# Side streams that run further in front: filters, convolutions and token sums placed anew in the Hyena stage of a single-core inference step

## The chip, the cores and the metric

One core of a Trainium2 chip runs the whole step. The metric is the device time of one execution in microseconds. The engines are named as in the profile: PE is the matrix engine, PEld its weight loads, DVE the vector engine, ACT the scalar engine, POOL and SP two further engines, of which POOL and SP here mostly issue DMAs. Each engine takes its instructions in one fixed order, and waits on semaphores for the others.

## The reference

One layer of a hybrid backbone for two groups of tokens: 128 prompt tokens and 512 sample tokens, 640 in all, 1024 channels, float32. What bears on the change is the Hyena branch:

```python
h = x * (1 + scale) + shift
z = h @ w_in                                   # 1024 -> 10240 columns
hy = short_conv(hy, conv_w, conv_b)            # 3 taps along the tokens
v_h, x1, x0 = jnp.split(hy, 3, axis=-1)

def hyena_long_conv(v_h, x1, x0, h_fwd, h_bwd, d_bias):
    u = v_h * x1
    ...
    uf = jnp.fft.rfft(u.astype(jnp.float32), n=n, axis=1)
    ff = jnp.fft.rfft(filt_full, n=n, axis=0)
    y = jnp.fft.irfft(uf * ff[None], n=n, axis=1)[:, :L].astype(u.dtype)
    return (y + u * d_bias) * x0
```

The filter (`filt_full`) comes from a small network with a decay. The other branch is neighbourhood attention for the samples and plain attention for the prompt. Both are gated, projected, merged, projected out and normalised.

## The kernel before

All products are done with operands split into a high and a low part (`split`: a copy on ACT makes the high part, a subtraction on DVE the low part), so one product is three passes of PE: high by high, low by high, high by low (`mm3`).

**The stage.** The change touches the stage from about 60 to 370 us. Its main stream is the projection `h @ w_in` in tiles of 128 output channels (`conv_tile`, in the profile `mm`, for PE 48 matmuls of 128x320) and in blocks of values (`v`, `ve`). The 1024 Hyena channels go in four quarters of two tiles. `quarter_head(q)` makes `u` (tile n) and `x1` (tile 8+n) and multiplies them; `quarter_tail(q)` makes `x0` (tile 16+n). A tile's way is: two of four PSUM banks (`mm_0`, `mm_1`) are filled by PE; ACT copies them out to a padded row `zs0` or `zs1`, in turn, with four copies (L481 to L485); ACT does the middle tap (L487) and DVE the two outer taps (L489, twice, reading `zs`). The next tile's copies into the same `zs` wait for the second of these DVE passes, and the next matmuls into the same banks wait for the copies.

**The side streams.** `filter_spectrum(q)` makes the filter of a quarter and its transform: five classes of rows (`fl`), decay on DVE (`sd`), split (`sh`, `sl`), transform as products with cosine and sine matrices (`fa`, `fb`, `fc`, `fd`, `fp`), sums into `F`. `long_conv(q)` transposes `u` (`ut`), splits it (`uh`, `ul`), transforms it (`c_X`, `s_X`, `p_X`), combines to `X` and multiplies with `F` (`W`). `long_conv_back(q)` splits the product (`ph`, `pl`), transforms back (`yb`), transposes (`yp`, `y`), and adds `u * d_bias` (L633, L642); then `gate_conv` multiplies by `x0` (`yu`). `token_sums(r)` does sums over the blocks of tokens for a later product (`ts`, split into `t1` to `t4`, sent to memory by POOL's DMA queue).

**What sets the order.** The generators are interleaved when the kernel is written: `weave(main, side, a, b)` takes b steps of the side stream for a steps of the main one, `braid` alternates two side streams, `along(main, side, 2)` takes one step of the side for two of the main one. From this written order the framework's scheduler makes each engine's order at build time by its own estimates, written order being priority; what a step waits for by data, and which buffer comes free, then decides. `tc.issue_after(ins)` puts an instruction behind another, `keep_in_program_order` holds a place. Rows of 128x640 come from a ring of nine (`yh`): `ts`, `t1` to `t4`, `x0` and `yu` all take theirs from it, so that a new `x0` row may have to wait for an old `ts` row. At the end of the quarters `hand_over` closes the pool in which `zs0` and `zs1` lie, and the values `v0` take that memory.

Of the kernel before, what the change touches and what calls it, by code (L numbers as in the profile page):

```python
# [2 lines left out]

# [9 lines left out]
ALU = mybir.AluOpType  # L13
# [32 lines left out]
def tile_hyena_natten_step(ctx: ExitStack, tc: tile.TileContext, a, o):  # L46
# [9 lines left out]
    def two(t):  # L56
        return t.rearrange("p (a b) -> p a b", a=2)
# [10 lines left out]
    def weave(main, side, n_main, n_side):  # L68
        done, taken = 0, 0
        for _ in main:  # L70
            done += 1
            while taken * n_main < done * n_side:
                if next(side, StopIteration) is StopIteration:
                    break
                taken += 1
        for _ in side:
            pass
# [22 lines left out]
    def split(dst_h, dst_l, src, eng=None):  # L100
        hi = nc.scalar.activation(dst_h, src, AF.Copy)  # L101
        return hi, (eng or nc.vector).tensor_tensor(dst_l, src, f(dst_h), op=ALU.subtract)  # L102
# [348 lines left out]
        nc.scalar.activation(x[:, 4:10:5], two(pp[:]), AF.Copy)  # L451
        yield

    N_FILTER = 11

    zss = []
    for i in range(2):
# [135 lines left out]
    def long_conv_back(q):  # L593
        us, ident, hyd, R, W = out[f"u{q}"], out["ident"], out[f"hyd{q}"], out[f"R{q}"], out[f"W{q}"]
        ab = hw.tile([P, 4, 256], F32, tag="plus", name=f"ab{q}")
        gd = hw.tile([P, 4, 256], F32, tag="minus", name=f"gd{q}")
        nc.vector.tensor_tensor(ab[:, 0:2], R[:, 0:6:5], R[:, 1:7:5], op=ALU.add)
        nc.vector.tensor_tensor(gd[:, 0:2], R[:, 2:8:5], R[:, 3:9:5], op=ALU.add)
        yield
        pq = W  # L600
        nc.vector.tensor_tensor(pq[:, 0:6:5], ab[:, 0:2], gd[:, 0:2], op=ALU.add)
        nc.vector.tensor_tensor(pq[:, 2:8:5], ab[:, 0:2], gd[:, 0:2], op=ALU.subtract)
        yield
        nc.vector.tensor_tensor(ab[:, 2:4], R[:, 0:6:5], R[:, 1:7:5], op=ALU.subtract)
        nc.vector.tensor_tensor(gd[:, 2], R[:, 7], R[:, 8], op=ALU.subtract)
        nc.vector.tensor_tensor(gd[:, 3], R[:, 2], R[:, 3], op=ALU.subtract)
        yield
        nc.vector.tensor_tensor(pq[:, 3:7:3], ab[:, 2:4], gd[:, 2:4], op=ALU.add)
        nc.vector.tensor_tensor(pq[:, 1:9:7], ab[:, 2:4], gd[:, 2:4], op=ALU.subtract)
        yield  # L610
        ye = hw.tile([P, 4, 256], F32, tag="e", name=f"ye{q}")
        yp = hw.tile([P, 256], F32, tag="minus", name=f"yep{q}")
        for g, rs_ in enumerate(((0, 2), (1, 3), (4,))):
            pb = aux(f"yb{q}_{g}")
            dst = ye[:, 2 * g : 2 * g + 2] if g < 2 else yp[:]
            for i, r in enumerate(rs_):
                s = pq[:, r : r + 6 : 5] if r < 4 else R[:, 4:10:5]
                ph = hw.tile([P, 2, 256], F32R, tag="shl", bufs=4, name=f"ph{q}_{r}")
                pl = hw.tile([P, 2, 256], F32R, tag="shl", bufs=4, name=f"pl{q}_{r}")
                split(ph[:], pl[:], s)  # L620
                for c in range(2):
                    mm3(
                        pb[:, i * 256 : i * 256 + 256], dftH[:, 1, r, c, :], dftL[:, 1, r, c, :],
                        ph[:, c], pl[:, c], start=(c == 0), stop=(c == 1),
                    )
            nc.scalar.activation(dst, two(pb[:]) if g < 2 else pb[:, :256], AF.Copy)
            yield
        outp = aux(f"yp{q}")
        for i in range(2):
            nc.tensor.transpose(outp[:, i * P : i * P + P], yp[:, i * P : i * P + P], ident)  # L630
        for i in range(2):
            up = us[i][:, :LP]
            nc.vector.scalar_tensor_tensor(  # L633
                up, up, hyd[:, i : i + 1], outp[:, i * P : i * P + P], op0=ALU.mult, op1=ALU.add
            )
        for i in range(2):
            n = 2 * q + i
            oy = aux(f"y{n}")
            for j, r in enumerate((0, 2, 1, 3)):
                nc.tensor.transpose(oy[:, r * P : r * P + P], ye[:, j, i * P : i * P + P], ident)  # L640
            uv = us[i][:, GAP:NG].rearrange("p (m r) -> p r m", r=4)
            nc.vector.scalar_tensor_tensor(  # L642
                uv, uv, hyd[:, i : i + 1], oy[:].rearrange("p (r m) -> p r m", r=4), op0=ALU.mult, op1=ALU.add
            )
            gate_conv(n)
            yield
# [48 lines left out]

    N_VALUES = 11

    AHEAD_OF = 5, 3

    SUMS = ("t2", "t3", "t1", "t4")  # L700

    def token_sums(r):
        def part(t, i, j):
            return f(t[:, 4 * i + 2 * r : 4 * i + 2 * r + 2, CS[j]])

        def step(dst, i, j, op):
            for t in (hH, hL):
                nc.vector.tensor_tensor(dst, dst, part(t, i, j), op=op)

        a_, b_ = (two(row(yhp, "yh", f"ts{r}{i}")) for i in range(2))  # L710

        def keep(name, t):
            at_ = 4 * SUMS.index(name) + 2 * r
            hi, lo = (row(yhp, "yh", f"{name}{r}{i}", F32R) for i in range(2))
            out["sums"] = split(two(hi), two(lo), t)[1].ins
            for i, x in enumerate((hi, lo)):
                nc.gpsimd.dma_start(tok_d[at_ + i], f(x))

        with tc.issue_after(out["sums"]) if r else nullcontext():
            ins = nc.vector.tensor_tensor(a_, part(hH, 0, 1), part(hL, 0, 1), op=ALU.add)  # L720
        if not r:
            tc.keep_in_program_order(ins)
        yield
        nc.vector.tensor_tensor(b_, part(hH, 0, 0), a_, op=ALU.subtract)
        nc.vector.tensor_tensor(b_, b_, part(hL, 0, 0), op=ALU.add)
        yield
        keep("t1", b_)
        yield
        nc.vector.tensor_tensor(a_, part(hH, 1, 1), a_, op=ALU.subtract)
        nc.vector.tensor_tensor(a_, a_, part(hL, 1, 1), op=ALU.add)  # L730
        yield
        keep("t3", a_)
        yield
        step(b_, 1, 1, ALU.add)
        yield
        keep("t2", b_)
        yield
        step(b_, 1, 0, ALU.subtract)
        yield
        keep("t4", b_)  # L740
        yield
# [10 lines left out]
    def chain(*gens):  # L752
        for g in gens:
            yield from g
# [4 lines left out]
    head = quarter_head(0)  # L759
    next(head)  # L760
    dft_consts()
    weave(head, filter_spectrum(0), 2 + NK, N_FILTER)
    pinned[0] = False
    sums = chain(token_sums(0), token_sums(1))

    def along(main, side, every):
        for i, _ in enumerate(main):
# [564 lines left out]
        yield from chain(until("slots_q"), attention_setup())  # L1332

    def filters():
        for q in range(3):
            yield from chain(until(f"used{q}"), filter_spectrum(q + 1))
            out[f"spectrum{q + 1}"] = True

    out["spectrum0"] = True
    weave(chain(along(quarters(), sums, 2), hand_over()), braid(convs(), filters()), AHEAD_OF[0], AHEAD_OF[1])  # L1340
    out["slots_r"] = left.enter_context(tc.tile_pool(name="slots_r", bufs=1))
    pinned[0] = True
# [384 lines left out]
```

## Time and profile before

| | us |
|---|---|
| median of 3 runs | 879.62 |
| lowest and highest | 879.43 and 879.99 |
| the profiled execution | 881.71 |
| its span, to which all times of the trace refer | 879.9 |
| PE busy in the span | 867.0 |
| DVE busy, ACT busy, POOL busy | 638.6, 450.3, 188.6 |
| mean granted TensorE clock | 0.997 of full |

The profiled execution lies 2.1 us above the median. Its span leaves out 1.8 us around it. Times in the trace are counted from the start of the span. Busy time of one instruction runs from its start to its end; consecutive instructions of one engine may overlap, so a busy share of 99% says that PE had nearly always something in it.

### The profile page before, as it was taken

What the parts mean: (1) busy time and instruction counts of PE and PEld (TensorE: products, weight loads), DVE (VectorE), ACT (ScalarE), POOL (GpSimd) and SP (SyncE); (2) the same over time, 40 slices, a digit from 0 to 9 for tenths busy, and PEclk for the clock granted to TensorE, in tenths of its full rate; (3) what the DMA queues carried; (4) which work ended last, traced back from release to release, by engine and by line L of the source; (5) the groups of instructions that cost most, each with busy time, mean ns of one, the idle gap of its engine ahead of it and who ended that gap; (6) DMA issues with size and microseconds to landing.
All of it is one profiled execution on the core that took longest, in us unless ns stands there. A gap on an engine that the chain in (4) does not pass through costs nothing.

```text
span 879.9 us, 17136 instructions
## 1 busy us (share of the span) xinstructions
PE 867.0 (99%) x6476; PEld 838.1 (95%) x6476; DVE 638.6 (73%) x1215; ACT 450.3 (51%) x956; POOL 188.6 (21%) x216
## 2 busy tenths in 40 slices
PE   8999999999999999999999999999999999999996
PEld 6899999999999999999999999999999999999885
DVE  4679896786786682588867787777777676666666
ACT  4396654545545535367565656656666622233200
POOL 0012211101101111147453434333453200000000
PEclk9999999999999999999999999999999999999998
DMA  8978876546656696998677668675854596445521
GB/s 311 402 175 232 226 212 150 139 108 169 144 119 146 161 224 143 332 299 230 182 214 187 196 163 251 142 219 162 226 143 113 189 337 206 164 151 187 188 91 53
DMA packets 75246, 169.09 MB, mean 192 GB/s; under 512 B 11003, under 2 KB 28667, under 8 KB 75164
## 3 DMA queue, kind: packets, MB, share of 16 engines
q1 hardware_dynamic: 56204, 123.06, 41.6%
q0 software_dynamic: 13632, 39.33, 23.2%
q10 hardware_dynamic: 5328, 5.61, 1.9%
q8 instruction: 51, 0.84, 0.4%
q14 instruction: 31, 0.25, 0.1%
HBM read 143.32 MB, written 23.99 MB: 190 GB/s over the span
## 4 chain that ended last, share of the span: by engine, by line
PE 96%; DVE 2%; ACT 1%; DMA 1%; issue 0%; POOL 0%; POOLq 0%; DVEq 0%; ACTq 0%
PE mm L182 36%; PE sp L1239 29%; PE out L1537 6%; PE v L661 5%; PE s L1045 2%; PE s L952 2%; PE pt L1036 2%; PE ve L672 1%; PE adaT L252 1%; DMA ra<-wall 1%; PE adaT L269 1%; PE fl L400 1%; PE yb L172 1%; PE yb L170 1%; PE yb L171 1%; PE fl L401 1%
## 5 line engine op out<-in xcount | busy, mean ns | idle before, releaser
L1239 PE MATMUL sp<-t,wb 128*128 128x320 f32 x1008 | 158.9, 311 | 0.0
L1239 PEld LDWEIGHTS sp<-t,wb 128*128 128x128 f32 x1008 | 150.1, 188 | 0.5 <-issue 0.5
L1239 PE MATMUL sp<-hH,wb 128*128 128x320 f32 x500 | 120.9, 313 | 0.0
L1239 PEld LDWEIGHTS sp<-hH,wb 128*128 128x128 f32 x500 | 86.0, 188 | 2.6 <-issue 2.6
L162 POOL DMA_DIRECT2D wl<-wall x34 | 30.4, 894 | 258.3 <-ACT wl L161 230.6
L182 PE MATMUL mm<-hH,wh 128*128 128x320 f32 x336 | 81.7, 313 | 0.7 <-ACT hH L328 0.5
L182 PE MATMUL mm<-hL,wh 128*128 128x320 f32 x336 | 80.8, 311 | 0.0
L182 PE MATMUL mm<-hH,wl 128*128 128x320 f32 x336 | 80.4, 310 | 0.4 <-DVE wl L102 0.4
L1239 PE MATMUL sp<-hL,wb 128*128 128x320 f32 x250 | 77.3, 309 | 0.0
L163 ACT ACTIVATE wh<-raw 128x1024 fp32r<-128x1024 f32 x34 | 36.1, 1062 | 48.8 <-PE mm L182 35.5
L1200 DVE TENSOR_TENSOR wb<-s,wb 128x512 fp32r<-128x512 f32 x63 | 45.0, 715 | 19.1 <-ACT wb L1192 18.9
L182 PEld LDWEIGHTS mm<-hH,wh 128*128 128x128 f32 x336 | 56.9, 188 | 1.9 <-ACT hH L328 0.8
L182 PEld LDWEIGHTS mm<-hH,wl 128*128 128x128 f32 x336 | 57.0, 188 | 1.1 <-DVE wl L102 0.9
L182 PEld LDWEIGHTS mm<-hL,wh 128*128 128x128 f32 x336 | 57.0, 188 | 0.9 <-DVE hL L329 0.5
L1007 POOL TENSOR_SCALAR edge<-edge,sm 128x320 f32<-128x320 f32 x32 | 43.3, 1511 | 61.7 <-DVE sm L1005 53.6
L1192 ACT ACTIVATE wb<-s 128x512 fp32r<-128x512 f32 x63 | 39.7, 631 | 32.0 <-PE sp L1239 20.4
L1007 POOL TENSOR_SCALAR p<-p,sm 128x384 f32<-128x384 f32 x32 | 50.0, 1658 | 24.2 <-DVE sm L1005 10.1
L1239 PEld LDWEIGHTS sp<-hL,wb 128*128 128x128 f32 x250 | 47.1, 188 | 0.0
L1537 PE MATMUL out<-woh,yhs 128*128 128x512 f32 (+1 forms) x176 | 45.8, 374 | 0.0
L1227 DVE TENSOR_TENSOR spare_hHp<-sp,yu 128x320 f32<-128x320 f32 x63 | 30.5, 484 | 18.4 <-PE sp L1239 11.4
L182 PE MATMUL mm<-yhs,wh 128*128 128x320 f32 x224 | 42.2, 310 | 0.0
L101 ACT ACTIVATE wh<-raw 128x1024 fp32r<-128x1024 f32 x15 | 15.8, 1059 | 44.8 <-PE mm L182 32.6
(415 smaller groups left out, 2266.0 us busy)
## 6 DMA issues: line engine op xcount, KB each, us to landing
raw<-wall SPq DMA_DIRECT2D x54, 512.0 KB, 3.8
wl<-wall POOLq DMA_DIRECT2D x34, 512.0 KB, 6.4
ra<-wall SPq DMA_DIRECT2D x21, 512.0 KB, 4.8
rb<-wall SPq DMA_DIRECT2D x40, 256.0 KB, 5.4
ada<-wada SPq DMA_DIRECT2D x16, 512.0 KB, 7.9
tm<-bias SPq DMA_DIRECT2D x16, 512.0 KB, 7.5
s<-wall SPq DMA_DIRECT2D x21, 256.0 KB, 5.0
s<-wall POOLq DMA_DIRECT2D x21, 256.0 KB, 4.3
```

What stands on the lines that cost most here:

```text
L162: nc.gpsimd.dma_start(wl, a["wall"][i], accum_op=ALU.add)
L163: nc.scalar.activation(wh, raw[:], AF.Copy)
L182: nc.tensor.matmul(ps[hf][:, :HALF], wt[k], x[:, hf * HALF : (hf + 1) * HALF], start=(i == 0 and k == 0), stop=(i == lead[2] and k == NK - ...
L661: nc.tensor.matmul(ps[t // 2][:, t % 2 * 256 : t % 2 * 256 + 256], x[:, k, P * t : P * t + P], wk, start=first and t % 2 == 0, stop=last, ...
L952: nc.tensor.matmul(dst[h], x[rows(h), qs], y[rows(h), ks], start=i == 0, stop=i == 2, skip_group_check=True)
L1007: nc.gpsimd.tensor_scalar_mul(pv, pv, sm[:, 2, c : c + 1])
L1036: nc.tensor.transpose(pt[:, i * P : i * P + P], ps[h][:, c : c + P], ident)
L1192: nc.scalar.activation(made[g][:, 0], block(g), AF.Copy)
L1200: nc.vector.tensor_tensor(made[g][:, 1], block(g), f(made[g][:, 0]), op=ALU.subtract)
L1227: nc.vector.tensor_tensor(c, dst, c if j == 3 else ps["u"], op=ALU.add)
L1239: nc.tensor.matmul(dst, wk, x(xi, k), start=j < 4 and k == 0 and i == 0, stop=k == 3 and i == 2, skip_group_check=True,)
L1537: ins = nc.tensor.matmul(dst, m[k][:, c0 : c0 + P], w[:, c : c + n], start=(first and k == 0), stop=(last and k == 5), skip_group_check=True,)
```

## The change

Four things are done; the amount of work is the same but for the order.

1. `AHEAD_OF` goes from 5, 3 to 2, 3: three steps of the side streams per two of the main stream, where it was three per five, until the side streams are used up or wait.
2. Of the first filter only 6 steps are woven into the first quarter's head; the rest of it becomes the first part of the stream `filters()`, and runs beside `convs()`.
3. `long_conv(0)` is no longer written behind the whole first filter; only its product with `F` needs that (`spectrum0` is set when the filter is done).
4. `token_sums(0)` and `token_sums(1)` are no longer written from the stage's start on: each starts when the way back of quarter 0 or 1 has reached its last step, and its first addition is put behind the last split (`pl`, the low part) of that way back.

```diff
@@ -1,5 +1,6 @@
 import math
 from contextlib import ExitStack, nullcontext
+from itertools import islice
 
 import numpy as np
 import concourse.bass as bass
@@ -451,7 +452,7 @@
         nc.scalar.activation(x[:, 4:10:5], two(pp[:]), AF.Copy)
         yield
 
-    N_FILTER = 11
+    N_FIRST = 6
 
     zss = []
     for i in range(2):
@@ -617,13 +618,15 @@
                 s = pq[:, r : r + 6 : 5] if r < 4 else R[:, 4:10:5]
                 ph = hw.tile([P, 2, 256], F32R, tag="shl", bufs=4, name=f"ph{q}_{r}")
                 pl = hw.tile([P, 2, 256], F32R, tag="shl", bufs=4, name=f"pl{q}_{r}")
-                split(ph[:], pl[:], s)
+                out[f"turned{q}"] = split(ph[:], pl[:], s)[1].ins
                 for c in range(2):
                     mm3(
                         pb[:, i * 256 : i * 256 + 256], dftH[:, 1, r, c, :], dftL[:, 1, r, c, :],
                         ph[:, c], pl[:, c], start=(c == 0), stop=(c == 1),
                     )
             nc.scalar.activation(dst, two(pb[:]) if g < 2 else pb[:, :256], AF.Copy)
+            if g == 2:
+                out[f"half{q}"] = True
             yield
         outp = aux(f"yp{q}")
         for i in range(2):
@@ -695,7 +698,7 @@
 
     N_VALUES = 11
 
-    AHEAD_OF = 5, 3
+    AHEAD_OF = 2, 3
 
     SUMS = ("t2", "t3", "t1", "t4")
 
@@ -712,14 +715,12 @@
         def keep(name, t):
             at_ = 4 * SUMS.index(name) + 2 * r
             hi, lo = (row(yhp, "yh", f"{name}{r}{i}", F32R) for i in range(2))
-            out["sums"] = split(two(hi), two(lo), t)[1].ins
+            split(two(hi), two(lo), t)
             for i, x in enumerate((hi, lo)):
                 nc.gpsimd.dma_start(tok_d[at_ + i], f(x))
 
-        with tc.issue_after(out["sums"]) if r else nullcontext():
-            ins = nc.vector.tensor_tensor(a_, part(hH, 0, 1), part(hL, 0, 1), op=ALU.add)
-        if not r:
-            tc.keep_in_program_order(ins)
+        with tc.issue_after(out[f"turned{r}"]):
+            nc.vector.tensor_tensor(a_, part(hH, 0, 1), part(hL, 0, 1), op=ALU.add)
         yield
         nc.vector.tensor_tensor(b_, part(hH, 0, 0), a_, op=ALU.subtract)
         nc.vector.tensor_tensor(b_, b_, part(hL, 0, 0), op=ALU.add)
@@ -759,9 +760,9 @@
     head = quarter_head(0)
     next(head)
     dft_consts()
-    weave(head, filter_spectrum(0), 2 + NK, N_FILTER)
+    first_filter = filter_spectrum(0)
+    weave(head, islice(first_filter, N_FIRST), 2 + NK, N_FIRST)
     pinned[0] = False
-    sums = chain(token_sums(0), token_sums(1))
 
     def along(main, side, every):
         for i, _ in enumerate(main):
@@ -1332,11 +1333,11 @@
         yield from chain(until("slots_q"), attention_setup())
 
     def filters():
-        for q in range(3):
-            yield from chain(until(f"used{q}"), filter_spectrum(q + 1))
-            out[f"spectrum{q + 1}"] = True
-
-    out["spectrum0"] = True
+        for q in range(4):
+            yield from chain(until(f"used{q - 1}"), filter_spectrum(q)) if q else first_filter
+            out[f"spectrum{q}"] = True
+
+    sums = chain(until("half0"), token_sums(0), until("half1"), token_sums(1))
     weave(chain(along(quarters(), sums, 2), hand_over()), braid(convs(), filters()), AHEAD_OF[0], AHEAD_OF[1])
     out["slots_r"] = left.enter_context(tc.tile_pool(name="slots_r", bufs=1))
     pinned[0] = True
```

The lines of the changed kernel carry numbers that are 1 higher than before up to L620, and 3 higher after L650; names carry a number at the end, which differs between the two.

**First place: PE at the second quarter's way there.** `ut1` are transposes of `u`, `c0_X1` and `s0_X1` the transform's products, `mm13` a projection tile. Before:

```order
L541 MATMUL ut1_0_1838<-pack2_380,u2_889 128x128
L541 MATMUL ut1_0_1838<-pack2_380,u3_1132 128x128
L182 MATMUL mm13_1_2104<-hH_85,wh13_2098 128x320
L182 MATMUL mm13_0_2103<-hL_87,wh13_2098 128x320
L182 MATMUL mm13_1_2104<-hL_87,wh13_2098 128x320
L182 MATMUL mm13_0_2103<-hH_85,wl13_2099 128x320
L182 MATMUL mm13_1_2104<-hH_85,wl13_2099 128x320
L541 MATMUL ut1_1_1845<-pack2_380,u2_889 128x128
L541 MATMUL ut1_1_1845<-pack2_380,u3_1132 128x128
L170 MATMUL c0_X1_1870<-uh1_0_1841,dftH_101 128x256
L170 MATMUL s0_X1_1871<-uh1_0_1841,dftH_101 128x256
L171 MATMUL c0_X1_1870<-ul1_0_1842,dftH_101 128x256
```

In the changed kernel, from the end of this way there (`p_X1`) through the next filter's first rows (`fl2`, `fa2`) to the next tile, `mm5`:

```order
L171 MATMUL p_X1_1601<-uh1_4_1597,dftH_101 128x256
L172 MATMUL p_X1_1601<-ul1_4_1598,dftH_101 128x256
L173 MATMUL p_X1_1601<-uh1_4_1597,dftL_102 128x256
L401 MATMUL fl2_0_1693<-w3h_2_1681,hid_93 128x512
L402 MATMUL fl2_0_1693<-w3l_2_1682,hid_93 128x512
L171 MATMUL fa2_1711<-sh2_0_1698,dftH_101 128x256
L401 MATMUL fl2_2_1729<-w3h_2_1681,hid_93 128x512
L402 MATMUL fl2_2_1729<-w3l_2_1682,hid_93 128x512
L183 MATMUL mm5_0_2253<-hH_85,wh5_2248 128x320
L183 MATMUL mm5_0_2253<-hL_87,wh5_2248 128x320
```

Before, matmuls of a tile stand between the transposes and between the products; now the whole way there, from `ut1_0` to `p_X1`, stands in one piece with no matmul of a tile in it (41 rows), and `mm5_0` begins behind it.

**The same place on DVE.** `x0_0` are the outer taps of tile 16, which read `zs0`; `t411` belongs to token sums 1, `pl_X0` and `mi_X0` to the first quarter's transform. Before:

```order
L564 TENSOR_TENSOR pl_X0_911<-e_X0_910,s1_X0_1052 128x512
L565 TENSOR_TENSOR mi_X0_912<-e_X0_910,s1_X0_1052 128x512
L102 TENSOR_TENSOR t411_1386<-ts11_1170,t410_1385 128x640
L489 SCALAR_TENSOR_TENSOR x0_0_1353<-zs0_105,pack2_380,x0_0_1353 128x641
L571 TENSOR_TENSOR X0_909<-pl_X0_911 128x2x256
L572 TENSOR_TENSOR X0_909<-pl_X0_911 128x2x256
L574 TENSOR_TENSOR X0_909<-mi_X0_912 128x2x256
L575 TENSOR_TENSOR X0_909<-mi_X0_912 128x2x256
L395 SCALAR_TENSOR_TENSOR hyd1_1260<-fz1_1257,pack2_380 128x2
L406 TENSOR_TENSOR sd1_0_1265<-fl1_0_1262,dec1_0_1246 128x512
L489 SCALAR_TENSOR_TENSOR x0_0_1353<-zs0_105,pack2_380,x0_0_1353 128x641
L489 SCALAR_TENSOR_TENSOR x0_1_1451<-zs1_109,pack2_380,x0_1_1451 128x641
```

Now, with `ts01` and `t401` of token sums 0, `ul1` splits of the second quarter's way there, and its sums `pl_X1`, `mi_X1`:

```order
L103 TENSOR_TENSOR ul1_1_1505<-ut1_1_1501,uh1_1_1504 128x256
L711 TENSOR_TENSOR ts01_1358<-ts01_1358,hH_85 128x640
L103 TENSOR_TENSOR ul1_2_1546<-ut1_2_1542,uh1_2_1545 128x256
L711 TENSOR_TENSOR ts01_1358<-ts01_1358,hL_87 128x640
L103 TENSOR_TENSOR ul1_3_1553<-ut1_3_1549,uh1_3_1552 128x256
L103 TENSOR_TENSOR t401_1618<-ts01_1358,t400_1617 128x640
L563 TENSOR_TENSOR pl_X1_1492<-e_X1_1491,c1_X1_1570 128x512
L564 TENSOR_TENSOR mi_X1_1493<-e_X1_1491,c1_X1_1570 128x2x256
L103 TENSOR_TENSOR ul1_4_1598<-ut1_4_1594,uh1_4_1597 128x256
L565 TENSOR_TENSOR pl_X1_1492<-e_X1_1491,s1_X1_1571 128x512
L566 TENSOR_TENSOR mi_X1_1493<-e_X1_1491,s1_X1_1571 128x512
L490 SCALAR_TENSOR_TENSOR x0_0_1472<-zs0_105,pack2_380,x0_0_1472 128x641
```

Before, both token sums are done ahead of `x0_0`, and `x0_0` stands in the first quarter's way there; now token sums 0 stand directly behind the first way back, in the second quarter's way there, and `x0_0` stands behind them. Its second pass stands seven rows further on, behind four sums of `X1` and the filter's `sd2_0`. On ACT the copies `zs0<-mm4_0`, which free the banks for `mm5_0`, wait for that pass.

**Second place: PE and DVE at the hand-over.** `yb3`, `yp3`, `y6` and `y7` are the last quarter's way back. PE now:

```order
L171 MATMUL yb3_2_3473<-ph3_4_3474,dftH_101 128x256
L172 MATMUL yb3_2_3473<-pl3_4_3475,dftH_101 128x256
L173 MATMUL yb3_2_3473<-ph3_4_3474,dftL_102 128x256
L633 MATMUL yp3_3485<-pack2_380,yep3_3416 128x128 x2
L643 MATMUL y6_3490<-pack2_380,ye3_3415 128x128 x4
L643 MATMUL y7_3502<-pack2_380,ye3_3415 128x128 x4
L183 MATMUL mm32_1_4025<-hH_85,wh32_4019 128x320
L183 MATMUL mm32_1_4025<-hL_87,wh32_4019 128x320
```

DVE now:

```order
L103 TENSOR_TENSOR pl3_4_3475<-X3_3243,ph3_4_3474 128x512
L636 SCALAR_TENSOR_TENSOR u6_2965<-u6_2965,hyd3_2584,yp3_3485 128x128
L636 SCALAR_TENSOR_TENSOR u7_3096<-u7_3096,hyd3_2584,yp3_3485 128x128
L472 TENSOR_TENSOR yu6_3757<-x0_6_3692,u6_2965 128x128
L645 SCALAR_TENSOR_TENSOR u6_2965<-u6_2965,hyd3_2584,y6_3490 128x4x128
L645 SCALAR_TENSOR_TENSOR u7_3096<-u7_3096,hyd3_2584,y7_3502 128x4x128
L490 SCALAR_TENSOR_TENSOR x0_7_3762<-zs1_109,pack2_380,x0_7_3762 128x641
L475 TENSOR_TENSOR yu6_3757<-x0_6_3692,u6_2965 128x64
L475 TENSOR_TENSOR yu6_3757<-x0_6_3692,u6_2965 128x8x7x8
L490 SCALAR_TENSOR_TENSOR x0_7_3762<-zs1_109,pack2_380,x0_7_3762 128x641
```

And before, on PE, where `mm65` is a projection tile of what follows the stage (`mm32`, the first tile of the queries, is done by then):

```order
L182 MATMUL mm65_1_4231<-hL_87,wh65_4225 128x320
L182 MATMUL mm65_0_4230<-hH_85,wl65_4226 128x320
L182 MATMUL mm65_1_4231<-hH_85,wl65_4226 128x320
L182 MATMUL mm65_0_4230<-hH_85,wh65_4225 128x320
L182 MATMUL mm65_1_4231<-hH_85,wh65_4225 128x320
L630 MATMUL yp3_3997<-pack2_380,yep3_3896 128x128 x2
L640 MATMUL y6_4002<-pack2_380,ye3_3895 128x128 x4
L640 MATMUL y7_4025<-pack2_380,ye3_3895 128x128 x4
L182 MATMUL mm65_0_4230<-hL_87,wh65_4225 128x320
L182 MATMUL mm65_1_4231<-hL_87,wh65_4225 128x320
L182 MATMUL mm65_0_4230<-hH_85,wl65_4226 128x320
L182 MATMUL mm65_1_4231<-hH_85,wl65_4226 128x320
```

Before, the last quarter's way back has matmuls of such tiles in it and after it; now `mm32_1` stands behind all of it. On DVE `x0_7` now stands behind the sums of `u6` and `u7` with the way back; before, both of its passes stand 40 rows ahead of that. The first copy of `v0` on ACT, which frees the bank for `mm32_1`, waits for the second pass of `x0_7`.

## The prediction

> **What bounds the kernel now.** I read the page first, its busy shares and the chain of work that ended last:
>
> ```profile
> PE 867.0 (99%) x6476; PEld 838.1 (95%) x6476; DVE 638.6 (73%) x1215; ACT 450.3 (51%) x956; POOL 188.6 (21%) x216
> PE 96%; DVE 2%; ACT 1%; DMA 1%; issue 0%; POOL 0%; POOLq 0%; DVEq 0%; ACTq 0%
> L162 POOL DMA_DIRECT2D wl<-wall x34 | 30.4, 894 | 258.3 <-ACT wl L161 230.6
> ```
>
> PE holds the end. The work is unchanged, so time can be won only where PE waits in the stage, and lost wherever PE comes to wait. The next view is PE's waits over the whole span, then PE's busy time in slices of 20 us (columns: length, then PE, PEld, DVE, ACT, POOL busy with counts, the granted clock, DMA share):
>
> ```profile
> PE s L952 <- ACT pts L1031: 0.6, 1, 0.6
> PE c_X L170 <- ACT uh L101: 0.6, 1, 0.6
> PE c_X L171 <- DVE ul L102: 0.5, 1, 0.5
> ...
> 160.00:180.00 20.00, 18.95 (x138) 18.55 (x137) 13.14 (x23) 11.14 (x27) 2.90 (x4) 1.00 0.53 125
> 320.00:340.00 20.00, 20.00 (x143) 20.00 (x142) 14.88 (x26) 11.46 (x24) 2.57 (x3) 1.00 0.83 184
> 380.00:400.00 20.00, 19.36 (x150) 18.12 (x150) 17.65 (x48) 13.82 (x40) 13.47 (x14) 1.00 0.84 252
> ```
>
> In the stage PE waits twice, both at the second way there (`c_X` for its splits): 0.6 and 0.5, which is the 1.05 missing in 160 to 180. The slice 380 to 400 misses 0.64, in the attention. So the change can win about 1.05, at most 1.7. DVE and ACT have idle time, but that is no help where one chain runs through both and PE has nothing else in its order.
>
> **Prices.** DVE's groups of the stage (60 to 372 us; busy, mean ns), then a stretch of DVE's timeline with starts and lengths, then ACT's groups, then PE's timeline:
>
> ```profile
> L489 DVE SCALAR_TENSOR_TENSOR x<-zs,pack,x 128x641 f32<-128x641 f32 x31 | 27.2, 880 | 3.4 <-ACT x L487 3.4
> L406 DVE TENSOR_TENSOR sd<-fl,dec 128x512 f32<-128x512 f32 x19 | 13.0, 686 | 9.7 <-PE fl L401 9.6
> L584 DVE TENSOR_TENSOR X<-X,F 128x2560 f32<-128x2560 f32 x4 | 11.3, 2818 | 0.0
> L642 DVE SCALAR_TENSOR_TENSOR u<-u,hyd,y 128x512 f32<-128x512 f32 x8 | 9.3, 1159 | 0.0
> L102 DVE TENSOR_TENSOR ul<-ut,uh 128x256 fp32r<-128x256 f32 x20 | 8.4, 418 | 3.2 <-ACT uh L101 3.2
> L102 DVE TENSOR_TENSOR t<-ts,t 128x640 fp32r<-128x640 f32 x8 | 6.5, 818 | 0.2 <-ACT t L101 0.2
> L581 DVE TENSOR_TENSOR W<-X,F 128x1280 f32<-128x1280 f32 x4 | 5.9, 1483 | 0.3 <-ACT X L570 0.3
> L708 DVE TENSOR_TENSOR ts<-ts,hL 128x640 f32<-128x640 f32 x4 | 3.3, 819 | 0.0
> L562 DVE TENSOR_TENSOR pl_X<-e_X,c_X 128x512 f32<-128x512 f32 x4 | 2.7, 686 | 8.0 <-PE c_X L172 8.0
> L571 DVE TENSOR_TENSOR X<-pl_X 128x512 f32<-128x512 f32 x4 | 2.7, 682 | 0.0
> L633 DVE SCALAR_TENSOR_TENSOR u<-u,hyd,yp 128x128 f32<-128x128 f32 x8 | 2.4, 344 | 16.6 <-PE yp L630 16.6
> ```
>
> ```profile
> 163.77 1.15 DVE L642 SCALAR_TENSOR_TENSOR u<-u,hyd,y 128x512 f32<-128x512 f32 x1
> 164.84 0.28 DVE L471 TENSOR_TENSOR yu<-x,u 128x128 f32<-128x128 f32 x1
> 165.04 1.16 DVE L642 SCALAR_TENSOR_TENSOR u<-u,hyd,y 128x512 f32<-128x512 f32 x1
> 166.10 1.42 DVE L474 TENSOR_TENSOR yu<-x,u 128x64 f32<-128x64 f32 x4
> ...
> 168.98 0.88 DVE L489 SCALAR_TENSOR_TENSOR u<-zs,pack,u 128x641 f32<-128x641 f32 x1
> ...
> 169.89 0.83 DVE L512 TENSOR_TENSOR u<-u,x 128x641 f32<-128x641 f32 x1
> ```
>
> ```profile
> L487 ACT ACTIVATE x<-zs,pack 128x641 f32<-128x641 f32 x15 | 14.1, 942 | 0.0
> L101 ACT ACTIVATE uh<-ut 128x256 fp32r<-128x256 f32 x20 | 7.9, 393 | 15.7 <-PE ut L541 15.7
> L484 ACT ACTIVATE zs<-mm 128x128 f32<-128x128 f32 x21 | 6.1, 290 | 0.0
> L101 ACT ACTIVATE t<-ts 128x640 fp32r<-128x640 f32 x8 | 6.0, 750 | 2.3 <-DVE ts L725 2.2
> L481 ACT ACTIVATE zs<-mm 128x128 f32<-128x128 f32 x21 | 5.6, 267 | 0.2 <-DVE u L489 0.2
> L483 ACT ACTIVATE zs<-mm 128x64 f32<-128x64 f32 x21 | 4.7, 225 | 0.0
> L677 ACT ACTIVATE v<-v 128x512 f32<-128x512 f32 x2 | 1.1, 596 | 2.5 <-PE v L661 2.5
> ```
>
> ```profile
> 169.46 0.28 PE L171 MATMUL s_X<-ul,dftH 128*128 128x256 f32 x1
> 169.58 0.28 PE L172 MATMUL s_X<-uh,dftL 128*128 128x256 f32 x1
> ...
> 170.68 0.31 PE L182 MATMUL mm<-hH,wl 128*128 128x320 f32 x1
> 170.83 0.31 PE L182 MATMUL mm<-hHp,wh 128*128 128x320 f32 x1
> ```
>
> PE starts a product of 256 columns every 0.12 and one of 320 every 0.147; I take transposes at 0.12 too, and 512 columns at 0.24. On DVE an operation that needs nothing of its forerunner starts 0.08 before the forerunner's end (163.77 + 1.15 against 164.84); one that reads its result starts behind the end (168.98 + 0.88 against 169.89).
>
> **Parts that I cost at nothing.** The first filter's later steps and the first convolution, moved beside each other in 60 to 150 us, still have tile matmuls between all their groups in PE's new order: those are the cover, and without it each split would show as the 0.5 to 0.6 above. POOL's sixteen stores of token sums move from before the stage's first third to behind the ways back, where weight loads share its queue: POOL waits 230.6 of 258.3 for ACT, so its queue is not what ends last. SP gets the filters' loads a little earlier; the reader of the sums is far behind.
>
> **First place (A), a loss.** In PE's new order 10 matmuls of `mm12`, then the whole second way there, `fl2` and one of `fa2` stand between the transposes `yp0` and `mm5_0`: 10 x 0.147 + 37 x 0.12 + 20 x 0.12 + 4 x 0.24 = 9.3, less 0.3 for the time that `yp0` takes to end, 9.0. All four banks are full, and `mm5_0` needs the copies of `mm4` out of them, which need `zs0`, which needs `x0_0`'s second pass on DVE. From the end of `yp0` DVE must do, in order: two L633, two L642, three sums `ts01`, five `ul1`, `t201`, `t401`, four `pl`/`mi`, the first pass of `x0_0`, a tiny one, four `X1`, `sd2_0`, the second pass. At full means: 0.69 + 2.32 + 2.46 + 2.09 + 1.64 + 2.74 + 0.88 + 0.1 + 2.73 + 0.69 + 0.88 = 17.2; with 0.08 less for each of 25 starts, 15.2. Then ACT: L481, an L487, L483, L484 = 1.72. Without any wait of DVE, `mm5_0` would come at 15.2 + 1.7 - 9.0 = 7.9 too late, or at 17.2 + 1.7 - 9.0 = 9.9.
>
> [...]
>
> DVE also waits, since splits go from PE over ACT to DVE and back. Worked step by step from the end of `yp0`: `fp1` ends at 3.0, ACT's copy of it 3.6, `uh1_0` 4.0, `ul1_0` 4.5; ACT's `t200` 4.8, `t201` 5.6; `ul1_1` 6.0; `ts01` with one more addition 6.7, `ul1_2` 7.1, the second addition 7.8; `uh1_3` stands behind two copies of `c0_X1`, `s0_X1` on ACT: 8.1; `ul1_3` 8.6; `t400` 8.9, `t401` 9.7; `pl`, `mi`, `ul1_4`, `pl`, `mi` 12.5; `x0_0` first 13.3; `X1` 15.8; `sd2_0` 16.4; second pass 17.3; ACT's four 19.0. So DVE waits some 2 us of it, and **A costs 19.0 - 9.0 = 10.0**. This lies near the end of 9.9; ends 7.9 and 12 (17.2 + 2 + 1.7 - 9.0).
>
> **Behind it (B).** `mm13_0` waits the same way for `x0_1`'s second pass: two `W1` (1.48 each), `sl2_0`, `yu0`, the first pass, `sd2_2`, L584 (2.82) and the second pass, some 9.5 behind `x0_0`, plus 0.8 on ACT, against 48 x 0.147 + 12 x 0.12 = 8.5 of PE behind `mm5_0`, which itself starts 1.7 behind `x0_0`. That leaves 0.1 to 0.7; I take 0.7, ends 0 and 1.5. Token sums 1, in the third quarter's way there, have values and `mm6` between on PE: 0, up to 1.5.
>
> **Hand-over (C), a loss.** `yb3_1`, `yb3_2`, `yp3`, `y6`, `y7` stand back to back, then `mm32_1`, which needs the bank of `v0`; `v0`'s copy needs the memory of `zs1`, so `x0_7`'s second pass. From `yp3`'s end DVE does two L633, L471, two L642, the first pass, `yu6` (two of the four at 166.10), the second pass: 0.69 + 0.28 + 2.32 + 0.88 + 0.71 + 0.88 = 5.8, or 5.3 with the early starts; then L677, 0.6. PE has 8 transposes meanwhile, 1.0, so 4.9 to 5.4 too late. The last splits and the copy ahead of `yp3` are uncovered too: 0.7 to 1.4. I take 5.3 + 1.4 = **6.7**, ends 4.9 and 7.9. In 320 to 340 before PE misses nothing (20.00).
>
> **Won.** The 1.05 of `c_X` in the old order goes, since the same splits now fall into A.
>
> **Sum.** 10.0 + 0.7 + 6.7 - 1.05 = +16.4, on a profiled execution of 881.7 (span 879.9), so 898.1 there. The median of the runs is 2.1 below that execution; on it 879.6 + 16.4 = 896.0.
>
> **Rivals.**
> 1. *Faster.* The waits do not appear since DVE is further ahead than I have it, and 1.05, at most 1.7, is won: 878 to 878.6. It decides at one point: `x0_0`'s second pass must end within 9.0 - 1.7 = 7.3 of `yp0`'s end, half of DVE's 15.2 of rows that stand between. For it speaks only that DVE has idle time earlier; but the rows behind L633 need `yp0`. The same must hold at C.
> 2. *The clock falls in the waits.* The last rows of the trace, PE's last matmul and then two slices:
>
> ```profile
> 871.32 0.28 PE L1537 MATMUL out<-woh,yhs 128*128 128x256 f32 x1
> ...
> 872.50:875.00 2.50, 0.00 (x0) 0.00 (x0) 2.33 (x8) 0.29 (x1) 0.00 (x0) 0.94 0.00 0
> 875.00:879.90 4.90, 0.00 (x0) 0.00 (x0) 1.48 (x3) 0.44 (x1) 0.93 (x2) 0.50 0.31 107
> ```
>
>    The clock is full until about 0.3 before 875.0 (mean 0.94 of 2.5 us), that is 3.1 after the last matmul's end at 871.6, then half. At A, PE is idle from `fl2_0`'s end to `fa2` (12.4 to 17.1 in the count above, 4.7); at C from `y7` to `mm32_1`, some 5.3. If the clock falls there and takes as long to come back, each costs half of 3.1 on a PE that is then fully loaded: 3.1 for both, 899.1; one alone 897.6. [...]
> 3. *One place only.* A alone: 879.6 + 10.0 + 0.7 - 1.05 = 889.3; C alone: 885.3 (6.7 - 1.05). Against it: both rest on orders that are fixed.
> 4. *No change within 0.2%* (1.8 us, about what a measurement of this kernel can tell): waits below 2.8 in sum, against 12.8 of lower ends.
>
> **Chances.** Forecast 0.53; clock 0.24; one place only 0.14; no change 0.03; faster 0.06, of which about half by over 0.2%. The likeliest gives 896. Range: lower ends 7.9 + 0 + 4.9 - 1.05 = 11.8 give 891.4; one place alone reaches down to 887 with A's lower end (7.9 + 0.7 - 1.05 = 7.5); upward, the sum with clock 899 and B, C at their upper ends 901. So 887 to 901. Faster by over 0.2% 0.04, within 0.05, slower 0.91.
>
> **What would show it.** Right: PE's waits list `mm` L183 for ACT L485 with 2 to 4 us at about 168, `fa` for ACT `sh`, `c_X` for `ul` and `uh` several times, and `mm` for L680 with 5 us at about 335 to 345; the slices there miss 10 and 7. Wrong: these slices full; or PE missing time in 60 to 150, where I cost the moved streams at nothing. What would break the number is a wait that I took as covered (the third quarter's way there), or token sums slower on DVE than 0.82.

## The result, and the profile after

The changed kernel takes 906.6 us (median of 4 runs, 905.81 to 907.39), the kernel before on the same chip 879.81 (879.43 to 880.14): 1.0305 times as long, 95% interval 1.0287 to 1.0323, 26.8 us slower. The direction was forecast, the size was not: 896.0 with 887 to 901 stood in the prediction.

The page of the changed kernel's profile (span 905.6, 25.7 longer), busy shares and the chain:

```profile
PE 876.0 (97%) x6476; PEld 844.5 (93%) x6476; DVE 638.0 (70%) x1215; ACT 450.9 (50%) x956; POOL 189.0 (21%) x216
PE 92%; DMA 2%; DVE 2%; issue 2%; ACT 1%; POOL 0%; SPq 0%; POOLq 0%; ACTq 0%
```

PE's part of the chain falls from 96% to 92%, so PE waits more; and its busy time grows by 9.0 us for the same 6476 matmuls, so they also run slower somewhere. PE's waits (total, times, longest):

```profile
PE mm L183 <- ACT v L680: 5.0, 1, 5.0
PE fa L171 <- ACT sh L102: 4.3, 1, 4.3
PE mm L183 <- DMA wl<-wall: 3.7, 1, 3.7
PE c_X L171 <- ACT uh L102: 1.8, 1, 1.8
PE mm L183 <- ACT mx L876: 1.6, 1, 1.6
...
PE fz L391 <- issue: 1.0, 1, 1.0
```

The first line is the hand-over (C), the second, fourth and sixth are the second way there (A). The third and fifth are a place that the prediction does not have; call it E. Time slices of 20 us show the three (PE's busy time is the second number, the granted clock the one before DMA share and GB/s):

```profile
140.00:160.00 20.00, 18.19 (x122) 17.51 (x122) 17.24 (x28) 12.39 (x22) 5.61 (x9) 0.91 0.71 195
160.00:180.00 20.00, 14.59 (x80) 13.17 (x79) 20.00 (x30) 8.74 (x18) 1.08 (x2) 0.83 0.21 78
...
340.00:360.00 20.00, 14.96 (x91) 14.72 (x92) 7.62 (x18) 6.47 (x15) 4.48 (x10) 0.83 0.71 226
360.00:380.00 20.00, 14.68 (x95) 13.94 (x94) 1.08 (x5) 7.45 (x14) 3.22 (x4) 0.94 0.92 233
380.00:400.00 20.00, 20.00 (x125) 20.00 (x124) 7.45 (x14) 5.83 (x12) 0.00 (x0) 0.89 0.58 177
```

In each of these slices the clock is below 1.00 too (0.83 to 0.94). To size the places I took the interval between each two starts of PE's matmuls and subtracted the usual interval of that width (0.147 us for 320 columns, 0.119 for 256, 0.233 for 512, 0.109 for 128). What is over by more than 0.2 us I count as a wait, the rest as slow clock. The line between the two is rough: starts at full clock have small gaps as well (0.3 of A's 1.7 in the kernel before).

| place, us from the start | waits | slow clock | the kernel before, same work, both |
|---|---|---|---|
| A, 150 to 180 | 9.5 | 3.2 | 1.7 |
| C, 335 to 355 | 6.7 | 2.0 | 0.0 |
| E, 372 to 390 | 5.9 | 2.3 | 0.0 |

That is 29.6 - 1.7 = 27.9. The same matmuls in both traces agree: the first of `fa` starts at 65.23 before and 64.26 after, the first of the attention's sums (`sp` from `hHp`) at 369.02 and 396.16, so 28.1 are lost between the two. Some 1.5 come back behind it (of this about 1.0 are waits of the attention at 397.9 to 398.8 that are gone), and 1.0 is the earlier start, which leaves the 25.7 of the span.

**A, in the trace of the changed kernel**, first PE, then DVE:

```profile
162.72 0.40 PE L402 MATMUL fl<-w3l,hid 128*128 128x512 f32 x1
167.39 0.58 PE L171 MATMUL fa<-sh,dftH 128*128 128x256 f32 x1 [4.27 <-ACT sh L102]
...
168.98 0.64 PE L183 MATMUL mm<-hH,wh 128*128 128x320 f32 x1 [0.16 <-ACT zs L485]
```

```profile
162.71 0.88 DVE L490 SCALAR_TENSOR_TENSOR x<-zs,pack,x 128x641 f32<-128x641 f32 x1
...
165.98 0.69 DVE L407 TENSOR_TENSOR sd<-fl,dec 128x512 f32<-128x512 f32 x1
166.58 0.88 DVE L490 SCALAR_TENSOR_TENSOR x<-zs,pack,x 128x641 f32<-128x641 f32 x1
```

`mm5_0` starts when the copy L485 is done, which comes behind `x0_0`'s second pass (ends at 167.5), as forecast. But PE's wait there is only 0.2 where the prediction looked for 2 to 4: its longest wait stands ahead of it, at `fa`, and at a clock of 0.50 `fa` (0.58 us; 0.28 for the first one at 64.26) and the two `fl` behind it took up what was left. DVE has no idle time in 160 to 180 (20.00 of 20).

**C.** `x0_7`'s second pass, `v`'s copy that waits for it, and `mm32_1`:

```profile
344.64 0.92 DVE L490 SCALAR_TENSOR_TENSOR x<-zs,pack,x 128x641 f32<-128x641 f32 x1
```

```profile
345.64 1.08 ACT L680 ACTIVATE v<-v 128x512 f32<-128x512 f32 x2 [4.94 <-DVE x L490]
```

```profile
346.30 0.63 PE L183 MATMUL mm<-hH,wh 128*128 128x320 f32 x1 [5.04 <-ACT v L680]
```

**E.** SP's loads of the hand-over, before:

```profile
304.09 1.80 SPq L63 DMA_DIRECT2D t<-tok_d  x4
...
322.39 14.41 SPq L63 DMA_DIRECT2D raw<-wall  x3
...
348.35 0.80 SPq L63 DMA_DIRECT2D t<-tok_d  x2
```

and after, with ACT's copies of the last of these weights and the two readers of `mm64` behind them:

```profile
346.19 1.84 SPq L64 DMA_DIRECT2D t<-tok_d  x4
...
350.59 0.90 SPq L64 DMA_DIRECT2D t<-tok_d  x2
...
354.88 1.27 SPq L64 DMA_DIRECT2D t<-tok_d  x2
357.34 2.75 SPq L64 DMA_DIRECT2D raw<-wall  x2
```

```profile
370.86 1.06 ACT L162 ACTIVATE wl<-raw 128x1024 fp32r<-128x1024 f32 x1 [10.12 <-DMA raw<-wall]
...
374.18 0.77 ACT L876 ACTIVATE mx<-mm 128x320 f32<-128x320 f32 x2
```

The first `mx` before:

```profile
350.02 0.77 ACT L875 ACTIVATE mx<-mm 128x320 f32<-128x320 f32 x2
```

Before, the raw weights of `mm65`, `mm56` and `mm57` start at 322 to 337, ahead of the loads of the second token sums (348), and 46 us lie between the first of the hand-over's loads and the first `mx` (304.1 to 350.0). After, it is 28 (346.2 to 374.2): the hand-over's loads start only at 345.8, when `x0_7` (second pass to 345.56) has let go of the pool; the second sums stand ahead of the weights; those start at 357.3 and are there at 370.9, with a DMA share of 1.02 to 1.13 in the slices of 352 to 370. ACT waits 10.1 us for them, and `mx`, which frees the banks, stands behind it on ACT.

### The profile page after: what moved, and what is told of

It reads as the page before. It is cut to its first block, busy times and chain, and to the rows that moved or that the text cites. A ratio compares the mean times of both kernels' runs of the same rounds, so it can differ in the third digit from the quotient of the medians.

```text
span 905.6 us, 17156 instructions
## 1 busy us (share of the span) xinstructions
PE 876.0 (97%) x6476; PEld 844.5 (93%) x6476; DVE 638.0 (70%) x1215; ACT 450.9 (50%) x956; POOL 189.0 (21%) x216
## 4 chain that ended last, share of the span: by engine, by line
PE 92%; DMA 2%; DVE 2%; issue 2%; ACT 1%; POOL 0%; SPq 0%; POOLq 0%; ACTq 0%
PE mm L183 33%; PE sp L1240 29%; PE out L1538 6%; PE v L664 5%; PE s L1046 2%; PE s L953 2%; PE pt L1037 2%; PE ve L675 1%; PE adaT L253 1%; DMA rb<-wall 1%; DMA wl<-wall 1%; DMA t<-tok_d 1%; PE yb L172 1%; PE adaT L270 1%; PE yb L173 0%
## 5 line engine op out<-in xcount | busy, mean ns | idle before, releaser
L183 PEld LDWEIGHTS mm<-hH,wh 128*128 128x128 f32 x336 | 58.0, 191 | 10.1 <-ACT v L680 5.3
L164 ACT ACTIVATE wh<-raw 128x1024 fp32r<-128x1024 f32 x34 | 36.1, 1060 | 59.4 <-PE mm L183 44.8
L162 ACT ACTIVATE wl<-raw 128x1024 fp32r<-128x1024 f32 x34 | 36.2, 1065 | 10.6 <-DMA raw<-wall 10.1
```

Of the source, the lines that this page charges most:

```text
L162: nc.scalar.activation(wl, raw[:], AF.Copy, scale=-1.0)
L164: nc.scalar.activation(wh, raw[:], AF.Copy)
L183: nc.tensor.matmul(ps[hf][:, :HALF], wt[k], x[:, hf * HALF : (hf + 1) * HALF], start=(i == 0 and k == 0), stop=(i == lead[2] and k == NK - ...
```

## The experiments

Four runs take single parts. The first two keep AHEAD_OF 2, 3.

**Late token sums undone.**

The sums are written at the stage's start again; cut to the main lines:

```diff
-        with tc.issue_after(out[f"turned{r}"]):
...
+        with tc.issue_after(out["sums"]) if r else nullcontext():
...
+    sums = chain(token_sums(0), token_sums(1))
...
-    sums = chain(until("half0"), token_sums(0), until("half1"), token_sums(1))
```

> The changed kernel with token sums written at the stage's start again, as before; AHEAD_OF 2, 3 and the split first filter stay. In PE's order the second way there then has matmuls of mm5 and mm13 between its groups, while the last way back still stands in one piece ahead of mm32_1. Theory 1 (three places; the first needs both the late sums and the faster side streams, the other two, x0_7 at the hand-over and the weights of mm64, need only the faster side streams): the 9.5 us of waits and 3.2 us of slow clock at 150 to 180 go, C and E stay: 906.6 - 11 = 895 to 896. Rival (late sums cause all three, since their stores and loads crowd the queues at the hand-over): back to 880.

Measured 901.26 us, 1.0236 (1.0222 to 1.0249). The rival is out; of A more stays than expected. Its waits:

```profile
PE mm L183 <- ACT v L680: 5.0, 1, 5.0
PE mm L183 <- DMA wl<-wall: 4.6, 2, 3.8
PE c_X L171 <- ACT uh L102: 1.9, 1, 1.9
```

`fa` no longer waits, but `c_X` still does: A falls from 12.7 to 4.9 (3.2 of waits, 1.6 of slow clock). C and E stay, and a wait of `yb` for `pl` on DVE (1.5) is new.

**AHEAD_OF 2, 3 alone, in the kernel before.**

```diff
-    AHEAD_OF = 5, 3
+    AHEAD_OF = 2, 3
```

> The kernel before with AHEAD_OF 2, 3 and nothing else. Theory 1: C and E appear at the hand-over as in the changed kernel, nothing at the second way there: 879.8 + 8.7 + 7.9 less about 1 = 895 to 896, like the run with old sums. Rival (late sums cause the waits): 880.

Measured 900.07 us, 1.0222 (1.0207 to 1.0237): C and E come from this one number. It is 4 to 5 us more than expected, partly since the last way back now also waits for its splits (1.5 of waits of `yb` for `pl` on DVE), partly from the second way there.

**The changed kernel with AHEAD_OF 5, 3.**

> The changed kernel with AHEAD_OF 5, 3 again; late sums and the split first filter stay. Theory 1: no stretch of over 2.1 us without tile matmuls is left in PE's order, so none of the three places waits: 878.5 to 880.5. Rival (the late sums burden DVE wherever they stand, in front of x0 rows that take their buffers): 885 to 891, with waits of mm for zs.

Measured 880.0 us, 0.9996 (0.9988 to 1.0005). None of the three places is in its trace; the wait of `c_X` that the kernel before has is gone too.

**Late token sums alone, in the kernel before.**

> The kernel before with the late token sums and nothing else. Theory 1: no wait of over 1 us; the 1.05 us of c_X at 168 may go, since x0_0 and the sums no longer stand where they did: 878.5 to 880.5. Rival as for the changed kernel with AHEAD_OF 5, 3: 885 to 891.

Measured 880.41 us, 1.0002 (0.9992 to 1.0013). The wait of `c_X` is gone, and a tile waits 1.6 for `mx`. So the late sums cost nothing by themselves: A in full needs both, the late sums and the side streams in front; with the early sums 4.9 of 12.7 are left.

**The split first filter alone, in the kernel before.**

> The kernel before with the split first filter and the first convolution not tied to its end, and nothing else. Prediction's cost of nothing for this part, and theory: 879.0 to 880.5. Rival (the fronted convolution crowds DVE and ACT in 60 to 150): 882 or above.

Measured 879.95 us, 0.9996 (0.9987 to 1.0004). This part costs nothing, as forecast.

Two runs ask for the cause of C and E.

**The last way there and back held until the hand-over.**

```diff
-            yield from chain(until(f"whole{q}"), long_conv(q), long_conv_back(q))
+            yield from chain(until(f"whole{q}"), until("slots_q" if q == 3 else f"whole{q}"), long_conv(q), long_conv_back(q))
```

> The changed kernel with the last quarter's way there and back held until the hand-over has opened its new pools (long_conv(3) waits for slots_q too); all else as changed. The last way back then has tiles mm32, mm40, mm64 and mm65 between its groups again, as before the change. Theory (C and the wait for the weights of mm56 come from a hand-over with no side stream left beside it): both go, the second way there stays as it is: 906.6 - 8.7 - 7.9 = 890. Rival (the late weights come from the stores and loads of the late sums): only C goes, 898.

Measured 893.47 us, 1.016 (1.0135 to 1.0186), its runs from 892.18 to 897.27. C and E are gone from the trace (1.7 of waits in 352 to 372 are left, `mm` for `mx`), A is there in full (9.5 and 3.0). Behind the stage its matmuls come 11.7 later than before (10.4 and 1.3 for an earlier start), which gives 891.7. Two of the four runs lie near it (892.2), the other two at 894.7 and 897.3, so the median is 1.8 above; why those two are longer stays open.

**Only the end of the last way back held behind `x0_7`.**

```diff
             yield from conv_tile(16 + n, out["x0"][n])
+            out[f"taps{n}"] = True
...
+        if q == 3:
+            yield from until("taps7")
         outp = aux(f"yp{q}")
```

> The changed kernel with the last part of the last way back (yp3, y6, y7 and the sums into u6, u7) held until x0_7's convolution is written, so that x0_7's taps come first on ACT and DVE; all else as changed. v0's copy then no longer waits for the way back, and matmuls of mm32 and mm40 stand in the way back. Theory (C is x0_7 behind the way back): C goes, and the loads of the hand-over start some 15 to 20 us earlier against PE's work, so the late weights go too: 890 to 892. Rival (the weights stay late): 898.

Measured 891.13 us, 1.0126 (1.0111 to 1.0141). The whole list of waits above 1 us is A and the kernel's start:

```profile
PE fa L171 <- ACT sh L102: 4.3, 1, 4.3
PE c_X L171 <- ACT uh L102: 1.8, 1, 1.8
PE adaT L270 <- POOL spare L285: 1.5, 1, 1.5
PE fz L391 <- issue: 1.1, 1, 1.1
```

So both C and E hang on one order: `x0_7`'s taps behind the last way back. The hold changes PE's order too (tile matmuls now stand in the way back), and the two effects are not told apart here.

**Weights ahead of the second sums on SP's queue.**

```diff
         for i in range(2):
             wraw(T_GA + i)
+        out["raw_ga"] = last[0]
...
+    with tc.issue_after(out["raw_ga"].ins):
         load_sums(1, SUMS[:1])
         sums_of_second = load_b(1)
         load_sums(1, SUMS[1:2])
```

> The changed kernel with the loads of the second token sums and of the second block (t2_1, t3_1, s2_1, rb1) put behind the raw weights of mm56 and mm57 on SP's queue, as they stand in the kernel before; all else as changed. The weights of mm56 can then start at 353, when their buffer comes free, in place of 357.3, and share the DMA engines with 2 MB less. Theory (their place in the queue and the crowd on the DMA engines make them late): of the 7.9 us at 372 to 390 some 5 to 6 go: 901. Rival (they are late because all loads of the hand-over start late, whatever their order): 906.

Measured 899.88 us, 1.0226 (1.0209 to 1.0243), 6.7 less than the changed kernel; expected were 5 to 6. Its SP queue and its waits:

```profile
352.36 7.22 SPq L64 DMA_DIRECT2D raw<-wall  x2
```

```profile
PE mm L183 <- ACT v L680: 5.0, 1, 5.0
PE fa L171 <- ACT sh L102: 4.3, 1, 4.3
...
PE mm L183 <- DMA wl<-wall: 0.7, 1, 0.7
```

C and A are untouched, E shrinks to 0.7. So E comes from the loads of the second sums standing ahead of the weights; that all of them start late only makes this order matter. Whether the place in the queue or the fuller DMA engines count for more stays open, since the edit changes both.

**The clock: useless matmuls in A's longest lull.**

```diff
+        if q == 2:
+            for _ in range(18):
+                nc.tensor.matmul(pa[:], hid[:, :P], w3h[:], start=True, stop=True, skip_group_check=True)
         dft_pair((pa[:, 0:256], pa[:, 256:512]), 0, *s0)
```

> The changed kernel with 18 useless matmuls of 128x512 more (4.2 us of PE at full clock), in the third filter, written into the bank of fa2 ahead of fa2's own first product, which overwrites it. They need nothing that is late, so they run in the first place's longest idle stretch, from fl2_0's end to fa2 (4.4 us at 163 to 167). The changed kernel's trace shows the clock at 0.50 from 166 to 172.6, 5 us of it with PE busy. Theory (a lull of PE lowers the clock, and the work behind the wait then pays): the clock stays full behind 166, some 1.8 us are won although PE has more to do: 904.8. Rival (the wait for x0_0 sets the time there and the clock is of no account): 906.6; rival (the added work is paid in full): 908 to 911.

Measured 906.36 us, 1.03 (1.0284 to 1.0315): not to be told from the changed kernel, with 4.2 us more of PE. Two slices of the changed kernel, then of this one:

```profile
165.00:170.00 5.00, 2.46 (x7) 1.74 (x8) 5.00 (x6) 2.32 (x6) 0.00 (x0) 0.60 0.10 26
170.00:175.00 5.00, 5.00 (x28) 5.00 (x28) 5.00 (x8) 1.56 (x2) 0.54 (x1) 0.72 0.26 92
```

```profile
165.00:170.00 5.00, 3.92 (x18) 3.04 (x18) 5.00 (x7) 2.33 (x6) 0.00 (x0) 1.00 0.09 26
170.00:175.00 5.00, 5.00 (x38) 5.00 (x37) 5.00 (x8) 1.56 (x2) 0.54 (x1) 1.00 0.20 70
```

Here the clock is 1.00 in both slices, and PE does 38 matmuls in 170 to 175 in place of 28. But it wins nothing: `mm5_0` now waits longer for the same copy.

```profile
169.60 0.41 PE L183 MATMUL mm<-hH,wh 128*128 128x320 f32 x1 [1.08 <-ACT zs L488]
```

It starts 2.39 behind the start of `x0_0`'s second pass (167.21); in the changed kernel it was 2.40 (166.58 and 168.98). Two more waits for DVE follow at 178 and 179 (0.8 and 0.3), since DVE has no idle time there in either kernel (5.00 of 5 from 175 to 180).

A with the added work comes to 11.9 against 12.7, but this 0.8 is not shown to be the useless matmuls'. The first fall of the clock, at 155.75 in the changed kernel, lies ahead of them, and it is not in this execution: the clock is 1.00 in every half microsecond from 150 to 175. `fz`, the next to wait behind that place, waits 1.4 here and 1.0 in the changed kernel. With weights first, where there are no useless matmuls, it waits 1.4 too, and A is 11.7; with the last way back held, where the clock is 0.50 from 155.0 to 158.0 and again from 165.5 to 171.5, it waits 1.2, with `x0_7` first 1.1. Counted from the first `fa`, the same matmul near 180 us comes at 114.92 here and at 114.89 with weights first, at 115.77 in the changed kernel, at 115.61 with the last way back held and at 116.25 with `x0_7` first. So by an estimate from these five the first fall costs 0.7 to 1.4, and the second, at A's longest lull, nothing that shows: `mm5_0` starts 2.40 behind the start of `x0_0`'s second pass in the changed kernel, at a clock of 0.50, and 2.39 here, at 1.00. The path over DVE sets the time there, as the first rival said.

Three runs put the parts together.

**Both undone: `x0_7` first and early token sums, AHEAD_OF 2, 3 kept.**

> The changed kernel with two things undone together: the last part of the last way back held until x0_7's convolution is written, and token sums at the stage's start again. AHEAD_OF 2, 3 and the split first filter stay. Theory (all of the loss is A plus the hand-over, and what is left of A without the late sums is the 3.2 us of waits and 1.6 of slow clock that the run with old sums showed at 160 to 170): 880 + 4.9 - 1.4 (the wait of c_X that the kernel before has too) = 883 to 884. Rival (AHEAD_OF 2, 3 costs something more beside these places): 886 or above.

Measured 883.33 us, 1.0038 (1.0024 to 1.0052): as expected, so no further cost of AHEAD_OF 2, 3 shows beside the places named.

**`x0_7` first, and the late sums also behind `x0_1` and `x0_3`.**

```diff
-    sums = chain(until("half0"), token_sums(0), until("half1"), token_sums(1))
+    sums = chain(until("half0"), until("taps1"), token_sums(0), until("half1"), until("taps3"), token_sums(1))
```

> The changed kernel with the same hold at the end, and with token sums 0 and 1 held, beside their own condition, until the convolutions of x0_1 and x0_3 are written. So x0_0 gets its row ahead of the sums, and on DVE both of its passes stand some 45 rows ahead of ts00; AHEAD_OF 2, 3 stays. PE's order then has a tile's matmuls between all groups of the second way there. Theory (A is x0_0 behind the late sums, not the late sums' work): the 12.7 us of A go as well as C and the late weights: 879 to 881. Rival (late sums crowd DVE in the second way there wherever x0_0 stands): 885 to 891.

Measured 880.40 us, 1.0007 (0.9998 to 1.0016). With all four points of the change in place and these two holds added, the loss is gone: A is `x0_0` standing behind the sums, not the sums' work.

**AHEAD_OF 4, 3 in the changed kernel.**

> The changed kernel with AHEAD_OF 4, 3. In PE's order the second way there has tile matmuls between its groups again, but the last way back stands in one piece of 4.6 us of PE ahead of mm32_1, as with 2, 3. Theory (it only matters whether the side streams are used up before the hand-over): C and the late weights as in the kernel before with 2, 3 alone, no A: 897 to 899. Rival (the loss grows with the ratio): 885 to 890.

Measured 907.47 us, 1.0318 (1.0302 to 1.0334): a miss for both. A is small (1.6 of waits in 140 to 180), but the hand-over loses more than with 2, 3:

```profile
PE mm L183 <- ACT v L680: 5.3, 1, 5.3
PE yb L171 <- ACT ph L102: 3.8, 1, 3.8
PE mm L183 <- DMA wl<-wall: 3.5, 1, 3.5
```

The last way there itself now ends so close to the hand-over that the first splits of the way back (`ph`) are bare too: 12.4 of waits and 4.4 of slow clock in 330 to 352. The loss does not fall with the ratio; what counts is which step of the side streams meets the end of the tiles.

No version beats the kernel before; those without the three places lie within 0.1% of it.

## Why the prediction was right or wrong

- **Bound and direction: right.** PE holds the end, little could be won, and the loss lies where PE's order had no tile matmuls.
- **A: right in place and chain, a little short in size.** By the prediction's own count `mm5_0` comes 19.0 behind the end of `yp0`; in the trace it is 19.9 (149.1 to 168.98). The waits in the table are 9.5 beside a forecast of 10.0, but the two are not the same measure: 3.2 of slow clock stand beside them. `x0_0` first brings A to nothing.
- **B: right at its lower end.** No wait of `mm13` for `zs` is in the list.
- **C: right.** Forecast 6.7, 6.7 of waits measured, in parts 5.2 behind the transposes (forecast 5.3) and 1.2 ahead of them (1.4); that the sums agree to the tenth is luck. `x0_7` first takes it away.
- **Won 1.05: right in the waits, not shown in the time.** The old waits of `c_X` at 168 are gone, as they are with AHEAD_OF 5, 3, with late sums alone and with the split filter alone; but these three take 0.9996, 1.0002 and 0.9996 of the kernel before, so no run shows that 1 us is won.
- **Failed: the parts that I cost at nothing.** "SP gets the filters' loads a little earlier; the reader of the sums is far behind" looked at SP's queue in the stage and stopped at its end. The hand-over's loads were not followed: the last way back, PE work that needs no loads, now stands ahead of them in place of beside them (28 us of cover in place of 46), and in SP's new order the second sums went ahead of the weights of `mm56`. E: 5.9 of waits and 2.3 of slow clock, 0 forecast. With the weights put ahead again and all else as changed the time is 899.88, inside the range.
- **Mis-sized: the clock.** It was a rival at 3.1 for two places with a chance of 0.24, not a term of the sum. It fell in all three places, and twice in A: 7.5 us of slow starts in sum. What of this is lost is estimated for A alone: 0.7 to 1.4 for the first fall; for the second nothing shows. I let it fall only in lulls over 3.1 us; the first fall in A comes behind one of 1.8. That it takes as long to come back was assumed; it was at 0.50 for 3.42 us once and for 6.82 or 6.83 three times.
- Against the range: its upper end took B and C at their upper ends but left A at 10.0; with A's own upper end of 12 it would have been 903, still below 906.6. The waits of A, C and E less the old ones of `c_X` are 9.5 + 6.7 + 5.9 - 1.4 = 20.7, or 900.5. What the time would be with the clock full throughout, no run shows.

## What to carry to other kernels

Work that needs no loads is what hides the loads of the next stage: a stream moved to the front is missing at its back, so follow every queue (SP's and the DMA engines' included) to the first reader after the stage's end. Where a shared row or pool ties a late step to an early one, look for the one instruction that frees it (`x0_0`, `x0_7`): holding what stands ahead of it cured here what the ratio 4, 3 did not. And price a lull of PE with the clock behind it (in A it fell to 0.50 behind lulls of 1.8 and 4.3 us), but only as far as PE is what ends next: where DVE was, a full clock won nothing that shows (906.36 against 906.6).

## What the runs showed of the hardware

In the trace of the changed kernel the granted clock falls from 1.00 to 0.50 at 155.75, 165.99, 343.49 and 377.62 and comes back to 1.00 at 159.17, 172.82, 350.31 and 384.45. So it is at 0.50 for 3.42 us once and for 6.82 or 6.83 three times. The distances of the falls are 10.24, 177.50 and 34.13, that is 3, 52 and 10 times 3.413 us. Cut in steps of that length, the stretch of A reads:

```profile
152.33:155.74 3.41, 1.60 (x12) 1.25 (x11) 2.39 (x4) 2.98 (x6) 1.30 (x2) 1.00 0.48 168
155.74:159.16 3.42, 3.42 (x17) 3.21 (x16) 2.71 (x6) 2.37 (x5) 0.69 (x2) 0.50 0.96 161
159.16:162.57 3.41, 2.42 (x20) 2.23 (x19) 3.38 (x6) 1.19 (x2) 1.08 (x2) 1.00 0.94 376
162.57:165.98 3.41, 0.54 (x3) 0.11 (x1) 3.41 (x7) 0.60 (x1) 0.00 (x0) 1.00 0.02 6
165.98:169.40 3.42, 1.86 (x4) 1.14 (x5) 3.42 (x5) 2.32 (x6) 0.00 (x0) 0.50 0.14 38
169.40:172.81 3.41, 3.41 (x14) 3.41 (x14) 3.41 (x7) 0.92 (x1) 0.54 (x1) 0.50 0.00 0
```

In the steps ahead of the four falls PE was busy for 1.60, 0.54, 1.18 and 1.03 of 3.41. Three steps at 1.00 with more of it, 2.29 (from 370.79), 2.42 (from 159.16) and 2.59 (from 336.67), were followed by another at 1.00. Of the steps at 0.50 those with 1.86, 0.61 and 1.59 were followed by another at 0.50, those with 3.41 or 3.42 by one at 1.00. These are the steps of one trace; what would hold between these numbers it does not show.

With the useless matmuls the wait of `c_X` near 154 is 1.8 as in the changed kernel, and the clock does not fall behind it. Which difference between the two executions decides this, no run shows.
